# A jump table on TensorE that picks narrower projections in a ragged self-attention kernel

## The chip, the cores and the metric

The kernel runs on one core of one Trainium2 chip. A core has five engines with an instruction stream each: TensorE (PE in the profile, its weight loads PEld), VectorE (DVE), ScalarE (ACT), GpSimd (POOL) and SyncE (SP). Each has a sequencer of its own that also runs register operations, branches and waits on semaphores. DMA engines move data between HBM and the on-chip memory, and they also bring each engine's instructions. The metric is the device time in microseconds (us) of one launch.

## The reference, cut to what matters

`x` holds 32 sequences of up to 512 rows of 512 numbers, 8 heads of 64. Each sequence has a length between 64 and 511, and rows from the length on come out as zero. The lengths are drawn once with a fixed seed; sorted in descending order they are 502, 447, 446, 436, 363, 357, 351, 347, 343, 333, 323, 315, 310, 261, 260, 257, 246, 230, 223, 220, 216, 183, 164, 152, 143, 140, 134, 119, 101, 86, 79, 75.

```python
for b in range(batch):
    seq_len = lengths[b]
    q, k, v = np.split(np.matmul(x[b, :seq_len], w_qkv), 3, axis=-1)
    # per head, scale = 1 / sqrt(64)
    scores = scale * np.matmul(q, k.transpose(0, 2, 1))
    attn = np.exp(scores - scores_max)
    attn = attn / (np.sum(attn, axis=-1, keepdims=True) + 1e-08)
    output[b, :seq_len] = np.matmul(attn, v)
```

## The kernel before, in words

**Head.** `before_loops` sorts the 32 sequences by length on the chip (lines 453 to 530), loads the weights and casts them to 16 bits (`w_r`), and computes the projections of the longest sequence. It also computes, for each loop, up to which pair of sequences it runs (`more`, `counts`, `ends`), and each engine reads these ends into registers (`read_ends`, line 686). DVE fills the masks `alive` and `lower`.

**Loops.** Sorted sequences are taken in pairs, 16 of them. `LOOPS` lists the padded lengths N = 512, 448, 384, 352, ..., 96. Each has one loop in the code, with a body of two positions, j = 0 and j = 1; it goes on while the pair's longer sequence needs more than the next smaller N. With these lengths loop 352 turns three times, 224 and 160 twice, and every other loop once. A loop's end (lines 1543 to 1553) advances registers on every engine and branches back.

**A position.** At position p TensorE works for two sequences at a time: the attention of sequence p, and the projections of sequence p + 1, whose rows lie transposed in `xT`, masked to zero past their length. The order of the steps within a position is written out by hand in `ORDER`, one list for each N (for some N one for each j). For N = 352 it is `L P D S0 S1 S2 V0 K0* V1 S3 S4 S5 A0 V2* K1* S6 S7 S8 A2 Q2* K3* Q1* S9 S10 S11 Q0 A4 Q3* K2* X A6`.

- S: scores, line 1155: matmuls on 64 rows, two heads side by side, N columns. ACT takes the exponential (line 1173).
- Q and K: projections of the next sequence through `project` (line 261): each block of 128 output rows is four matmuls that add up over c = 0 to 3, each N columns wide. They are 32 matmuls a position for every N. ACT (marked `*`) or DVE copies the result (line 1202).
- V (and W): its values, line 272 (1109), four matmuls of 512 columns each.
- A: attention times values, line 1244, many matmuls of 65 columns; DVE divides (lines 1254 to 1263) into `out_nat`.
- L, P, D, X: masks, casts on POOL (line 332), the load of a later sequence, and the transposition of the next `xT` by DMA.

For N of 128 and 96 the Q, K and V steps of the second position stand in a branch (`skip`, line 1459), so that the last sequence projects nothing after it.

**Waits.** `plan_waits` derives from the steps' reads and writes which semaphore each step waits for; PSUM's eight banks are dealt out by `allotted`. A step's instructions are emitted by `emit` and `issue` (the waits at line 1470). In the body each step is emitted once, in the order of the list, for all engines. The width of a projection is N, whatever the length of the next sequence, which is at most N.

Of the kernel before, what the change touches and what calls it, by code (L numbers as in the profile page):

```python
# [17 lines left out]
P = 128  # L18
# [5 lines left out]
class Op:  # L24
# [6 lines left out]
    writes: tuple = ()  # L31
    dma: bool = False
    skip: bool = False


def plan_waits(head, bodies, entries, rare):
# [122 lines left out]
def kernel(  # L159
# [95 lines left out]

        return 1 < tiles(N) and N <= tiles(N) * P - P // 2

    def project(dst, xT, w0, N, part=range(NC)):

        for c in part:  # L260
            last = nc.tensor.matmul(  # L261
                dst[:, 0:N],
                w_r[:, c, w0 : w0 + P],
                xT[:, c, 0:N],
                start=(c == 0),
                stop=(c == NC - 1),
            )
        return last
# [74 lines left out]
    def before_loops():  # L343
# [336 lines left out]
        def read_ends(e, part=None):  # L680
            def load():
                eng = EN[e]
                words = COUNTS // 4
                for g in range(words) if part is None else [part]:
                    packed = eng.alloc_register(f"packed{e}{g}")
                    eng.reg_load(packed, ends_i[0:1, g : g + 1])
                    for v in range(len(LOOPS) - 1):
                        word, bit = counted(v)
                        if word == g:
                            reg = of(ends[v], e)  # L690
                            if bit:
                                eng.reg_alu(reg, packed, bit, op=ALU.logical_shift_right)
                            if bit < 15:
                                eng.reg_alu(reg, reg if bit else packed, 31, op=ALU.bitwise_and)
# [113 lines left out]
        def twos(source):  # L808
# [83 lines left out]
            ("edge", "slen"),  # L892
            ("lower",),
        )
        read_ends("ACT", 2)
        shorten("wk", w_k, D, 0, "POOL")
        shorten("wk", w_k, D, 1, "POOL")
# [77 lines left out]
    def position(N, j, at, ring):  # L975
# [18 lines left out]
        def op(*args, **kw):  # L994
            ops.append(Op(*args, **kw))
# [193 lines left out]
        def qk(name, m0, is_q, act):  # L1189
            k = ring.pop(0)  # L1190
            bank = banks[k]
            ms = slice(m0, m0 + gm)
            buf = (q_bufs if is_q else k_bufs)[o]

            def matmuls():
                for m in range(gm):
                    w0 = (m0 + m) * P + (0 if is_q else D)
                    last = project(bank[:, m * N : (m + 1) * N], xT, w0, N)
                return last

# [8 lines left out]
            op(low, "PE", matmuls, (f"xT{o}",), (f"bk{k}",), skip=ends)  # L1209
# [253 lines left out]
    def issue(v, j, k, op, instead=None):  # L1463
# [14 lines left out]
        elif op.name in sems and last is not None:  # L1478
            last.then_inc(sems[op.name], 16 if op.dma else 1)

    with tc.tile_critical():
        started = [k for k, op in enumerate(head) if op.name in ("row", "col", "wv0", "wv2")]
        for k in started:
            emit("head", 0, k, head[k])
        for name, amount in lead.items():
            amount -= name in ahead
            if amount and name in owner:
                (nc.sync if owner[name] == "DVE" else EN[owner[name]]).sem_inc(
                    sems[name], unit(name) * amount
                )  # L1490
# [22 lines left out]
        here["until"] = nc.sync.alloc_register("until")  # L1513
        for k, op in enumerate(head):
            if k not in started:
                emit("head", 0, k, op)

        for v, N in enumerate(LOOPS):
            for e, eng in EN.items():
                for base, amount in sorted(fixed[v, e], key=lambda f: (f[0] != "posold", f)):  # L1520
                    reg = regs[e][base, amount]
                    if base == "posold":
                        eng.reg_mov(reg, regs[e]["posin", amount])
                        continue
                    eng.reg_mul(reg, rare_pair[e] if base == "rarein" else pair, entered[base])
                    eng.reg_add(reg, reg, amount)
            for k, op in enumerate(entries[v]):
                emit(v, None, k, op)
            for e in final:
                EN[e].reg_sub(final[e], of(ends[v], e), 1)  # L1530
            body, after = f"loop_{N}", f"after_{N}"
            nc.br_lt(pair, ends[v], on_true=body, on_false=after)
            with nc.body(body):
                hints = {}
                for e in ("ACT", "DVE", "POOL", "SP"):
                    EN[e].reg_alu(leave[e], pair, final[e], op=ALU.is_ge)
                    hints[e] = EN[e].mark_branch_hint_location(leave[e])
                p = nc.snap(pair, min_val=0, max_val=B // 2 - 1)
                here.update({e: p * 2 for e in EN}, pair=p, pairs=pair)
                for j in range(2):  # L1540
                    for k, op in enumerate(bodies[v][j]):
                        emit(v, j, k, op)
                nc.regs_add(pair, pair, 1)
                nc.regs_add(own_pair, own_pair, 1)
                if shared(N):
                    for e, reg in rare_pair.items():
                        EN[e].reg_add(reg, reg, 1)
                for e, eng in EN.items():
                    for (base, amount), reg in regs[e].items():
                        if base in raised and (base != "rare" or shared(N)):  # L1550
                            eng.reg_add(reg, reg, raised[base])
                for e, eng in EN.items():
                    back = eng.br_lt(pair, ends[v], on_true=body, on_false=after)
# [41 lines left out]
```

## Time and profile before

| | us |
|---|---|
| median of 3 runs (338.18 to 339.72) | 338.18 |
| span of the profiled execution, first to last instruction | 336.7 |
| TensorE busy | 322.2 |
| ScalarE busy | 264.5 |
| VectorE busy | 210.0 |
| GpSimd busy | 103.6 |
| Q and K projections (line 261), busy | 145.5 |
| V projections (line 272), busy | 72.3 |
| attention times values (line 1244), busy | 74.2 |
| scores (line 1155), busy | 61.2 |

The profiled execution has no time of its own beside its span; its distance to the median of the runs is 1.5 us. In the profile's rows a group reads "line engine operation out<-in xcount | busy us, mean ns of one | idle time of the engine before them and what ended it". Matmuls overlap each other in the pipeline, so a matmul's duration is longer than its distance from the next: four matmuls of 512 columns take 1.04 us from the start of the first to the end of the last, not four times 380 ns. A row of the timeline gives start, time from the first start to the last end, and what ran. The rows of a table by stretches give, after the stretch, its length and the busy time of each engine.

### The profile page before, as it was taken

The page shows a single profiled execution, that of the slowest core. Times are in us where ns is not written, and L with a number is a line of the kernel's source. Part 1 is how long each engine was busy: PE and PEld are TensorE (multiplying, and loading weights), DVE is VectorE, ACT ScalarE, POOL GpSimd, SP SyncE. Part 2 cuts the span into 40 slices and gives each one's busy share as a digit, 9 for nine tenths or more (in the row PEclk, how much of TensorE's full clock was granted, in tenths as well). Part 3 has the DMA queues.
Part 4 walks back from the last instruction along what each step waited for, and adds up shares of the span by engine and source line. Part 5 has one row for each costly group of instructions (what it writes and reads, how often), then busy time and mean ns, then how long its engine had stood idle before and what let it go on. Part 6 is the DMA issues. An engine that isn't in the chain of part 4 may idle for free.

```text
span 336.7 us, 10690 instructions
## 1 busy us (share of the span) xinstructions
PE 322.2 (96%) x3832; PEld 200.0 (59%) x3832; DVE 210.0 (62%) x654; ACT 264.5 (79%) x416; POOL 103.6 (31%) x149
## 2 busy tenths in 40 slices
PE   7999999999999999999999999999999999999881
PEld 4444545554555556556556656665677777678760
DVE  6676666666666564465455457665776656867764
ACT  5388799898978879989989988788567678777651
POOL 5546040504030320330231253043222244244321
PEclk9999999999999999999999999999999999999998
DMA  6974994484637946957947848969946966977671
GB/s 218 391 270 108 324 177 145 121 305 116 207 51 237 318 142 228 288 173 277 300 140 275 239 140 321 258 173 341 262 139 182 204 193 169 207 229 210 219 196 71
DMA packets 72124, 72.08 MB, mean 214 GB/s; under 512 B 41872, under 2 KB 41872, under 8 KB 72080
## 3 DMA queue, kind: packets, MB, share of 16 engines
q1 hardware_dynamic: 72032, 71.52, 71.9%
q8 instruction: 24, 0.39, 0.5%
q14 instruction: 20, 0.16, 0.2%
q10 hardware_dynamic: 48, 0.00, 0.0%
HBM read 28.32 MB, written 33.55 MB: 184 GB/s over the span
## 4 chain that ended last, share of the span: by engine, by line
PE 91%; DVE 3%; DMA 3%; issue 1%; SPq 0%; POOL 0%; ACT 0%; POOLq 0%
PE banks L261 38%; PE banks L272 18%; PE banks L1244 17%; PE banks L1155 16%; PE banks L1109 2%; DMA xT<-x 1%; DMA x_nat<-in_x_dram 1%; DVE out_nat L1263 1%; DVE rcp L1260 1%; PE banks L732 0%; DVE rcp L1254 0%; SPq L609 0%; DVE kT L781 0%; ACT et L1173 0%; DVE x L327 0%
## 5 line engine op out<-in xcount | busy, mean ns | idle before, releaser
L1173 ACT ACTIVATE et<-banks 128x704 f16<-128x704 f32 (+7 forms) x260 | 195.6, 826 | 31.7 <-PE banks L1155 30.3
L261 PE MATMUL banks<-xT,w_r 128*128 128x352 f16 (+11 forms) x1024 | 145.5, 287 | 1.4 <-DMA xT<-x 1.2
L332 POOL TENSOR_TENSOR x<-x_nat,mask 128x512 f16<-128x512 f32 x85 | 86.2, 1039 | 182.9 <-DVE mask L998 170.7
L261 PEld LDWEIGHTS banks<-xT,w_r 128*128 128x128 f16 x1024 | 85.4, 98 | 41.8 <-issue 7.4
L1244 PEld LDWEIGHTS banks<-v_aug,et 128*128 128x128 f16 x1792 | 66.4, 98 | 21.3 <-issue 7.2
L1244 PE MATMUL banks<-v_aug,et 128*128 128x65 f16 x1792 | 74.2, 194 | 0.7 <-ACT et L1173 0.7
L272 PE MATMUL banks<-w_r,xT 128*128 128x512 f16 x284 | 72.3, 380 | 0.6 <-DVE xT L741 0.5
L1263 DVE TENSOR_TENSOR out_nat<-banks,rcp 128x256 f32<-128x256 f32 (+1 forms) x136 | 64.1, 472 | 6.8 <-DMA out_dram<-out_nat 2.2
L1155 PE MATMUL banks<-qz,kT 64*128 64x352 f16 (+11 forms) x640 | 61.2, 298 | 2.9 <-DVE out_nat L1263 2.5
L1254 DVE RECIPROCAL rcp<-banks 128x4 f32<-128x4 f32 (+1 forms) x136 | 25.0, 184 | 44.3 <-PE banks L1244 42.8
L1202 DVE CAST qz<-banks 128x352 f16<-128x352 f32 (+5 forms) x44 | 25.3, 575 | 26.3 <-PE banks L261 25.8
L1155 PEld LDWEIGHTS banks<-qz,kT 64*128 64x128 f16 x640 | 22.6, 94 | 31.8 <-issue 23.4
L272 PEld LDWEIGHTS banks<-w_r,xT 128*128 128x128 f16 x284 | 23.7, 97 | 27.2 <-issue 5.2
L1218 DVE CAST v_aug<-banks 128x512 f16<-128x512 f32 x41 | 28.2, 692 | 16.7 <-PE banks L272 16.6
L1202 ACT CAST kT<-banks 128x352 f16<-128x352 f32 (+5 forms) x58 | 27.6, 478 | 10.2 <-PE banks L261 9.0
L1202 ACT CAST qz<-banks 128x352 f16<-128x352 f32 (+5 forms) x47 | 22.2, 477 | 6.0 <-PE banks L261 4.3
L1202 DVE CAST kT<-banks 128x512 f16<-128x512 f32 (+4 forms) x33 | 19.4, 590 | 7.3 <-PE banks L261 6.9
L1260 DVE TENSOR_TENSOR rcp<-rcp,v_aug 128x4 f32<-128x4 f32 (+1 forms) x108 | 19.6, 181 | 3.7
L1218 ACT CAST v_aug<-banks 128x512 f16<-128x512 f32 x26 | 15.6, 602 | 6.6 <-PE banks L272 6.6
L1074 DVE TENSOR_SCALAR v_aug<-alive 128x24 f16 (+3 forms) x32 | 7.7, 239 | 6.5 <-issue 6.5
L1341 POOL MEMSET kT<- 128x128 f16 (+1 forms) x8 | 1.7, 218 | 28.8 <-PE banks L1155 28.8
L418 PE MATMUL banks<-h_ones 128*128 128x128 f16 (+2 forms) x34 | 5.7, 349 | 1.9 <-POOL h_ones L408 1.9
(81 smaller groups left out, 84.0 us busy)
## 6 DMA issues: line engine op xcount, KB each, us to landing
x_nat<-in_x_dram SPq DMA_DIRECT2D x12, 768.0 KB, 5.5
out_dram<-out_nat SPq DMA_DIRECT2D x12, 768.0 KB, 4.0
x_nat<-in_x_dram SPq DMA_DIRECT2D x14, 512.0 KB, 3.8
x_nat<-in_x_dram SPq DMA_DIRECT2D x7, 1024.0 KB, 6.9
out_dram<-zeros SPq DMA_DIRECT2D x12, 512.0 KB, 5.6
out_dram<-out_nat SPq DMA_DIRECT2D x12, 512.0 KB, 4.5
out_dram<-out_nat SPq DMA_DIRECT2D x4, 1024.0 KB, 4.9
out_dram<-zeros SPq DMA_DIRECT2D x12, 256.0 KB, 5.5
```

The costliest lines, as they stand in the source:

```text
L261: last = nc.tensor.matmul(dst[:, 0:N], w_r[:, c, w0 : w0 + P], xT[:, c, 0:N], start=(c == 0), stop=(c == NC - 1),)
L272: last = nc.tensor.matmul(pv, xT[:, c, t * P : (t + 1) * P], w_r[:, c, 2 * D : 3 * D], start=(c == 0), stop=(c == NC - 1),)
L332: return engine.tensor_tensor(out=x16, in0=x32, in1=live.broadcast_to([P, D]), op=ALU.mult)
L1074: return nc.vector.tensor_scalar(out=v_bufs[o][:, t0:t1, :, HD], in0=table[:, bass.ds(at("DVE") + (j + 1), 1), t0:t1] .rearrange("p o t -> ...
L1155: last = nc.tensor.matmul(psc[par][:, x * wide : x * wide + N], kT[r, i, c0 : c0 + P], qz[r, i, 0:N], start=True, stop=True,)
L1173: return nc.scalar.activation(out=et[:, :, x0:x1, 0:N], in_=got.rearrange("p j (x q) -> p j x q", q=wide)[:, :, x0:x1, 0:N], func=AF.Exp, ...
L1202: return copy_on(act)(out=buf[:, ms, 0:N], in_=bank[:, 0 : gm * N].rearrange("p (m q) -> p m q", q=N),)
L1218: return copy_on(act)(out=v_bufs[o][:, t, :, 0:HD], in_=bank.rearrange("p (h d) -> p h d", d=HD))
L1244: last = nc.tensor.matmul(pav[:, g, qt, :], e_bufs[e][:, c0 + qt * P : c0 + (qt + 1) * P], v_aug[:, kt, h, :], start=(kt == 0), stop=(kt = ...
L1254: return nc.vector.reciprocal(out=rcp, in_=pav[:, :, :, HD])
L1260: return nc.vector.tensor_tensor(out=rcp, in0=rcp, in1=rows, op=ALU.mult)
L1263: return nc.vector.tensor_tensor(out=o_t[:, 0:n, h0 * HD : (h0 + heads) * HD].rearrange("p t (g d) -> p g t d", d=HD), in0=pav[:, :, :, 0:HD],
```

## The change

**A word for each pair.** Nine small DVE operations in the head compute, for each sequence, how many steps of 16 columns the length of the next one lies below its loop's N, at most 3, and pack the two numbers of a pair into one word of `variants`. Two POOL memsets clear the tables. TensorE reads the first word at the end of the head into a register; each second position reads the word of the next pair.

**A jump table in each position.** `emit_position` takes the place of the loop over a position's steps. All engines but TensorE get their steps as before. On TensorE the steps up to the first Q or K block that stands behind some other TensorE step are emitted once; then a `Switch` with four bodies, each of which holds every TensorE step from that block to the last Q or K block (S, V and A steps between them included); then the rest. In body v the matmuls of Q and K for c = 1, 2, 3 are 16v columns narrower than N, while c = 0 keeps the full width, so that every column is written. The columns left out belong to rows of `x` that are zero. Blocks ahead of the `Switch` keep the full width. Positions whose Q and K steps stand in a branch (second positions of 128 and 96) have no `Switch`.

The `Switch` is a jump through a register: a stride times the number of the variant, added to the first body's place. [...] 

```diff
-    def project(dst, xT, w0, N, part=range(NC)):
+    def project(dst, xT, w0, N, part=range(NC), live=None):
         for c in part:
+            width = live if live and c else N
             last = nc.tensor.matmul(
-                dst[:, 0:N],
+                dst[:, 0:width],
                 w_r[:, c, w0 : w0 + P],
-                xT[:, c, 0:N],
+                xT[:, c, 0:width],
...
+    STEP, VARIANTS, FIELD = 16, 4, 2
+    variants = const.tile([P, B // 2 + 1], I32)
...
+        op("kept0", "POOL", lambda: pool.memset(kept, 0), ("order",), ("kept",))
+        op("variants0", "POOL", lambda: pool.memset(variants, 0), ("order",), ("variants",))
+        whole = small("whole", "DVE", ...)      # length + 15
+        op("kept", "DVE", ...)                  # >> 4
+        narrow = small("narrow", "DVE", ...)    # loop of each pair, from `more`
+        wide = small("wide", "DVE", ...)
+        loop_of = small("loop_of", "DVE", ...)
+        loop_at = small("loop_at", "DVE", ...)  # N / 16
+        spare = small("spare", "DVE", ...)      # N / 16 - kept of the next sequence
+        least_of = small("least_of", "DVE", ...)  # at most 3
+        op("variants", "DVE", ...)              # second * 4 + first
...
+        op("word", "PE", lambda: nc.tensor.reg_load(here["variants"], variants[0:1, 0:1]), ("variants",))
...
-                    last = project(bank[:, m * N : (m + 1) * N], xT, w0, N)
+                    last = project(bank[:, m * N : (m + 1) * N], xT, w0, N, live=here["live"])
...
+    def emit_position(v, j):
+        ops, N = bodies[v][j], LOOPS[v]
+        mine = [k for k, op in enumerate(ops) if op.eng == "PE"]
+        blocks = [k for k in mine if ops[k].blocks]
+        first = next((k for k in blocks if any(not ops[i].blocks for i in mine if i < k)), None)
+        if first is None or ops[first].skip:
+            first = last = len(ops)
+        else:
+            last = blocks[-1] + 1
+        here["live"] = N
+        for k, op in enumerate(ops):
+            if op.eng != "PE" or k < first:
+                emit(v, j, k, op)
+        which, word = of(variant, "PE"), here["variants"]
+        def following():
+            if j:
+                nc.tensor.reg_load(word, variants[0:1, bass.ds(here["pair"] + 1, 1)])
+        if first == len(ops):
+            return following()
+        if j:
+            nc.tensor.reg_alu(which, word, FIELD, op=ALU.logical_shift_right)
+        else:
+            nc.tensor.reg_alu(which, word, 2**FIELD - 1, op=ALU.bitwise_and)
+        chosen = nc.snap(variant, min_val=0, max_val=VARIANTS - 1)
+        for at in nc.tensor.Switch(chosen, VARIANTS):
+            here["live"] = max(N - at * STEP, STEP)
+            for k in range(first, last):
+                if ops[k].eng == "PE":
+                    emit(v, j, k, ops[k])
+        following()
+        for k in range(last, len(ops)):
+            if ops[k].eng == "PE":
+                emit(v, j, k, ops[k])
...
-                    for k, op in enumerate(bodies[v][j]):
-                        emit(v, j, k, op)
+                    emit_position(v, j)
```

More of the change, by code (lines that the diff above doesn't have):

```diff
@@ L33 @@
     skip: bool = False
+    blocks: bool = False
 def plan_waits(head, bodies, entries, rare):
@@ L894, in before_loops @@
         )
+        kept = const.tile([P, B + 2], I32, name="h_kept")
+        op("kept0", "POOL", lambda: pool.memset(kept, 0), ("order",), ("kept",))
+        op("variants0", "POOL", lambda: pool.memset(variants, 0), ("order",), ("variants",))
+        whole = small(
+            "whole",
+            "DVE",
+            lambda t: dve.tensor_scalar(
+                out=t, in0=slen, scalar1=float(STEP - 1), scalar2=None, op0=ALU.add
+            ),
+            ("slen",),
+            (P, B),
+            I32,
+        )
@@ new lines, in before_loops @@
+        op(
+            "kept",
+            "DVE",
+            lambda: dve.tensor_scalar(
+                out=kept[:, 0:B],
+                in0=whole,
+                scalar1=STEP.bit_length() - 1,
+                scalar2=None,
+                op0=ALU.logical_shift_right,
+            ),
+            ("whole", "kept"),
+            ("kept",),
+        )
+        passed_by = [[(448 - M) // 32 for M in LOOPS[1:] if LOOPS[LOOPS.index(M) - 1] - M == d] for d in (32, 64)]
+        assert passed_by[0] == list(range(3, COUNTS)) and passed_by[1] == [0, 2]
@@ new lines, in before_loops @@
+        narrow = small(
+            "narrow",
+            "DVE",
+            lambda t: dve.tensor_reduce(
+                out=t, in_=more[:, 3:COUNTS, :].rearrange("p k j -> p j k"), axis=AX.X, op=ALU.add
+            ),
+            ("more",),
+            (P, B // 2),
+        )
+        wide = small(
+            "wide",
+            "DVE",
+            lambda t: dve.tensor_tensor(out=t, in0=more[:, 0, :], in1=more[:, 2, :], op=ALU.add),
+            ("more",),
+            (P, B // 2),
+        )
@@ new lines, in before_loops @@
+        loop_of = small(
+            "loop_of",
+            "DVE",
+            lambda t: dve.scalar_tensor_tensor(
+                out=t, in0=wide, scalar=2.0, in1=narrow, op0=ALU.mult, op1=ALU.add
+            ),
+            ("wide", "narrow"),
+            (P, B // 2),
+        )
+        loop_at = small(
+            "loop_at",
+            "DVE",
+            lambda t: dve.tensor_scalar(
+                out=t,
+                in0=loop_of,
+                scalar1=float(32 // STEP),
+                scalar2=float(LOOPS[-1] // STEP),
+                op0=ALU.mult,
+                op1=ALU.add,
+            ),
+            ("loop_of",),
+            (P, B // 2),
+        )
@@ new lines, in before_loops @@
+        spare = small(
+            "spare",
+            "DVE",
+            lambda t: dve.tensor_tensor(
+                out=t,
+                in0=loop_at.unsqueeze(2).broadcast_to([P, B // 2, 2]),
+                in1=kept[:, 1 : B + 1].rearrange("p (j two) -> p j two", two=2),
+                op=ALU.subtract,
+            ),
+            ("loop_at", "kept"),
+            (P, B // 2, 2),
+        )
+        least_of = small(
+            "least_of",
+            "DVE",
+            lambda t: dve.tensor_scalar(
+                out=t, in0=spare, scalar1=float(VARIANTS - 1), scalar2=None, op0=ALU.min
+            ),
+            ("spare",),
+            (P, B // 2, 2),
+        )
@@ L895, in before_loops @@
+        op(
+            "variants",
+            "DVE",
+            lambda: dve.scalar_tensor_tensor(
+                out=variants[:, 0 : B // 2],
+                in0=least_of[:, :, 1],
+                scalar=float(2**FIELD),
+                in1=least_of[:, :, 0],
+                op0=ALU.mult,
+                op1=ALU.add,
+            ),
+            ("least_of", "variants"),
+            ("variants",),
+        )
         read_ends("ACT", 2)
@@ L1513 @@
         here["until"] = nc.sync.alloc_register("until")
+        here["variants"] = nc.tensor.alloc_register("variants")
+        variant = nc.alloc_registers("variant", engines=[mybir.EngineType.PE])
         for k, op in enumerate(head):
```

2 lines of the change are left out of this document (1 added, 1 removed).

## The prediction

> **What bounds the kernel now.** I read the page first (busy shares, the granted clock, the queues, the chain that ended last), then the groups of instructions by line with shapes kept apart, then the table by stretches, and last TensorE's own order of time in the loop of 352.
>
> ```profile
> span 336.7 us, 10690 instructions
> PE 322.2 (96%) x3832; PEld 200.0 (59%) x3832; DVE 210.0 (62%) x654; ACT 264.5 (79%) x416; POOL 103.6 (31%) x149
> PEclk9999999999999999999999999999999999999998
> q8 instruction: 24, 0.39, 0.5%
> PE 91%; DVE 3%; DMA 3%; issue 1%; SPq 0%; POOL 0%; ACT 0%; POOLq 0%
> PE banks L261 38%; PE banks L272 18%; PE banks L1244 17%; PE banks L1155 16%; PE banks L1109 2%; DMA xT<-x 1%; DMA x_nat<-in_x_dram 1%; DVE out_nat L1263 1%; DVE rcp L1260 1%; PE banks L732 0%; DVE rcp L1254 0%; SPq L609 0%; DVE kT L781 0%; ACT et L1173 0%; DVE x L327 0%
> ```
>
> TensorE is the bound: busy 96%, 91% of the chain, at the full clock, and line 261, the Q and K projections that the change shortens, is the largest share of the chain (38%). So time that TensorE gains or loses inside a loop is nearly time of the kernel.
>
> The next rows give the cost of a column, the state of one stage, and how tight its other engines are.
>
> ```profile
> L261 PE MATMUL banks<-xT,w_r 128*128 128x352 f16 x192 | 33.6, 313 | 0.0
> L261 PE MATMUL banks<-xT,w_r 128*128 128x512 f16 x96 | 23.0, 379 | 0.0
> core 0: us, PE busy (x) PEld busy (x) DVE busy (x) ACT busy (x) POOL busy (x), PEclk, DMA share, GB/s
> 121.34:194.50 73.16, 73.16 (x842) 42.91 (x840) 37.69 (x108) 65.74 (x115) 18.42 (x19) 1.00 0.74 227
> ```
>
> A column costs (379 - 313) / 160 = 0.41 ns. The stretch is the loop of 352: three turns, six positions, 12.19 us each. ACT is at 90% there, so it can follow a faster TensorE only a little.
>
> **What is removed.** With the fixed draw, sorted, the next length gives these variants v (16v columns left out), two positions a pair: loop 512: 3, 3; 448: 0, 3; 384: 1, 2; 352: 0, 0, 1, 1, 2, 2; 320: 3, 3; 288: 1, 2; 256: 1, 2; 224: 0, 0, 2, 3; 192: 2, 3; 160: 1, 1, 2, 3; 128: 2; 96: 1 (in the last two only the first position has a jump). That is 30 jumps: 5 to variant 0, 25 to another. A position has 32 projecting matmuls, 24 of them shortened, so one unit of v is 24 x 16 = 384 columns or 0.158 us. Blocks that stand ahead of the first other TensorE step keep full width (K1, Q1 of 384's first position; K0, K2 of 224; K0 of 192's second). With these taken off, the units add up to 46.5: 46.5 x 0.158 = 7.4 us. As ACT and DVE must follow, I count 6 us, with 0 and 7.4 as ends.
>
> **What is added on TensorE's sequencer.** Ahead of the variants come a register operation, the two values of the stride, a multiplication, an addition and the jump.
>
> ```profile
> L692 PEldq ALU_OP  x3: 36/36/36, 14.6 to 15.0; - x3
> L694 PEldq ALU_OP  x3: 36/36/36, 14.5 to 14.9; - x3
> L1553 PEldq COMPARE_BRANCH  x2: 214/222/231, 145.3 to 169.7; - x2
> L1553 PEldq COMPARE_BRANCH  x3: 67/67/74, 60.3 to 120.9; - x3
> L686 PEldq TENSOR_LOAD <-ends_i x3: 311/318/499, 13.0 to 17.2; - x3
> ```
>
> The six operations of L692 and L694 start between 14.5 and 15.0 us: one in 0.1 us, whatever its 36 ns of work. The two taken back edges in the loop of 352 took 214 and 231 ns, the first three that fell through 67 to 74. So the entry is about 6 x 0.1 + 0.22 = 0.8 us of sequencer time. The exit is another taken jump (0.22 us), and each second position reads the next word (0.31 to 0.50 us).
>
> What covers this is the work already queued on TensorE when its sequencer reaches the jump. In the loop of 352 the order is S0 S1 S2 V0, then the variants from K0 on:
>
> ```profile
> 145.10 0.71 PE L1244 MATMUL banks<-v_aug,et 128*128 128x65 f16 x18
> 145.75 0.62 PE L1155 MATMUL banks<-qz,kT 64*128 64x352 f16 x6
> 146.31 1.04 PE L272 MATMUL banks<-w_r,xT 128*128 128x512 f16 x4
> 147.18 0.76 PE L261 MATMUL banks<-xT,w_r 128*128 128x352 f16 x4
> 157.30 0.71 PE L1244 MATMUL banks<-v_aug,et 128*128 128x65 f16 x18
> 157.94 0.62 PE L1155 MATMUL banks<-qz,kT 64*128 64x352 f16 x6
> 158.50 1.04 PE L272 MATMUL banks<-w_r,xT 128*128 128x512 f16 x4
> 159.37 0.76 PE L261 MATMUL banks<-xT,w_r 128*128 128x352 f16 x4
> L1470 PEldq EVENT_SEMAPHORE  x8: 51/51/51, 121.3 to 194.6; - x8
> ```
>
> The sequencer handles its separate semaphore wait just ahead of S0; from there it issues S and V0 in some 0.2 us (my estimate from the back edge at 145.3, which it has reached while the A matmuls of 145.10 still run). In a first position it restarts about at 145.75, so 1.2 us of matmuls stand before K0 at 147.18; in a second it can run on about when A starts at 157.30 and has up to 1.7 us before K0 at 159.37. Mean 1.45 us: the 0.8 us of entry alone are hidden, with 0.65 us left. Without that cover they would be 30 x 0.8 = 24 us. The exit and the load stand behind full projections (four matmuls of 352 are 0.6 us) and cost nothing or, where few are left, some tenths: 15 loads x 0.1 = 1.5 us; ends 0 and 15 x 0.5 = 7.5.
>
> **The term that decides: code that has to be fetched.** Each variant is a copy of 112 of the 140 matmuls of a 352 position (all but S0 to S2, V0 and the last A6), 224 instructions and more with the weight loads, and four stand one behind the other. The page's row of the instruction queue shows code streaming in while TensorE runs: 24 packets, 0.39 MB, 16 KB each. TensorE runs 2 x 3832 instructions; less the repeats (two turns of 352 at 561, one each of 224 and 160 at about 176 matmuls and as many loads) that is 6,190 different ones, and 0.39 MB over them is 63 bytes each: every piece of 16 KB, some 260 instructions, is fetched once, and a repeated turn fetches nothing. Its price: 0.5% of 16 engines' 336.7 us is 27 us, or 1.1 us a packet, with nobody waiting. A jump past the next piece asks for a packet nobody has ordered. No row shows one. From below it costs the packet alone, 1.1 us. The nearest rows with a start-up are the two smallest loads:
>
> ```profile
> col<-in_lengths_dram ACTq DMA_DIRECT2D x1, 0.2 KB, 1.9
> row<-in_lengths_dram SPq DMA_DIRECT2D x1, 8.0 KB, 2.0
> ```
>
> 2.0 us to land 8 KB, mostly start-up, plus a packet's 1.1 us gives 3.1 us, which I take since a demanded fetch has both. From above: two start-ups and a packet, 2 x 2.0 + 1.1 = 5.1 us.
>
> Variant 0 follows the jump directly; I take it as already on its way, at no cost. For the other 25, 3.1 - 0.65 = 2.45 us of TensorE standing still. Some comes back: a 352 position needs (32 x 352 + 12 x 512 + 12 x 352) x 0.41 ns + 72 x 0.03 us = 11.0 us of its 12.19 (the two row halves of the S matmuls run together), so up to 1.2 us are small waits on ACT and DVE, which catch up during a stall. I give back 0.25, leaving 2.2 us: 25 x 2.2 = 55 us. Ends: 25 x (1.1 - 0.65 - 0.45) = 0 and 25 x (5.1 - 0.65) = 111 us.
>
> [...]
>
> **Back edges.** Four are taken (352 twice, 224 and 160). A turn now holds some ten pieces and touches about eight. If the head is gone, a back edge costs a fetch less the matmuls queued, about 2 us; if not, nothing as now. I take half: 4 us, ends 0 and 4 x 4.5 = 18.
>
> **The start.** DVE gets nine small operations, two memsets go to POOL and a load to TensorE.
>
> ```profile
> 14.39 0.28 DVE L886 TENSOR_TENSOR lower<-h_edge,h_slen 128x128 f32<-128x128 int32 x1
> 16.12 0.69 DVE L781 CAST qz<-banks 128x512 f16<-128x512 f32 x1 [1.45 <-PE banks L261]
> 14.59 1.91 POOL L709 CAST w_r<-w_k 128x512 f16<-128x512 f32 x3 [0.74 <-DMA w_k<-in_w_qkv_dram]
> 22.08 0.99 PE L1155 MATMUL banks<-qz,kT 64*128 64x512 f16 x6 [0.35 <-DVE kT L781]
> ```
>
> Nine at 0.16 to 0.28 us are 1.5 to 2 us, behind "lower", where DVE idles 1.45 us; POOL waits 0.74 us for w_k anyway and TensorE 0.35 us for kT. Zero; were that cover gone, 0.5 us.
>
> **Sum.** Span 336.7 - 6 + 1.5 + 55 + 4 + 0 = 391.2 us. The median of the runs, 338.18, stands 1.5 us over this span, so 392.7; I say 392.
>
> **Rivals.** (1) *The pieces are there already.* If TensorE's memory is filled several pieces ahead, or a fetch takes under the 0.65 us of cover, no jump waits: 338.2 - 6 + 1.5 = 333.7, down to 331. For it: back edges over two pieces cost nothing. Against: 24 packets for 24 pieces show no large lead, and a packet alone takes 1.1 us. Deciding point: the fetch equals the cover; each 0.1 us over it costs 2.5 us, and at 0.25 us over it the gain is gone.
> (2) *Only the sequencer's work is seen.* No fetch waits, but cover is shorter outside 352 and 0.3 us of each of 30 jumps shows: 338.2 - 6 + 9 + 1.5 = 343.
> (3) *The clock falls as well.* In the tail TensorE's last matmul starts near 330.1:
>
> ```profile
> 330.07 0.18 PEld L1244 LDWEIGHTS banks<-v_aug,et 128*128 128x128 f16 x4 [0.21 <-ACT et L1173]
> 330.50:336.70 6.20, 0.00 (x0) 0.00 (x0) 1.58 (x5) 0.00 (x0) 0.45 (x1) 0.81 0.22 86
> ```
>
> A mean of 0.81 over 6.2 us fits half clock for the last 2.4, so about 4 us of idleness suffice. [...] Stalls of 2.45 us stay below; at 4 us each a few us of half speed follow, say 1.5 us lost a time: 25 x (4 - 0.25 + 1.5) = 131, with the other terms 469; where half of them fall so, about 431.
>
> **Chances.** Forecast (fetches wait, 340 to 430) 0.70; rival 1 0.15; rival 2 0.06; rival 3 0.09. The range 339 to 435 leaves out rival 1 and part of rival 3 (0.05). The forecast's own range is 360 to 430. A measurement of this kernel tells 0.5%, 1.7 us, from no change: faster 0.15 (rival 1), same 0.04 (the forecast's low end, where a fetch costs hardly more than its cover), slower 0.81.
>
> **What would show it.** Right: instruction packets well over 24; TensorE idle 2 to 3 us just before the first Q or K block behind V0 in about 25 positions and not in those with v = 0; the loop of 352 longer in its second and third turn than in its first (v = 0, 0); matmuls of L261 in forms 16 to 48 columns narrower; DVE's Q copies at most 0.5 us later. Wrong: gaps of under 0.5 us there (rivals 1 and 2), equal gaps in all 30 (the jump, not the fetch), a PEclk row with digits of 5 to 7 (rival 3).

## The result, and the profile after

The changed kernel takes 557.98 us (median; 551.33 to 563.5) against 338.24 before: a ratio of 1.642 (95% interval 1.633 to 1.651). Slower was forecast, by 54 us; it is 220 us, outside the stated range. The profiled execution is the slowest of the four, at 563.5 us (span 561.7), 1% above the median; its rows are read for where the time lies.

The page of the changed kernel, the lines that answer to those shown of before:

```profile
span 561.7 us, 11070 instructions
PE 382.8 (68%) x3832; PEld 224.8 (40%) x3833; DVE 213.8 (38%) x663; ACT 267.9 (48%) x416; POOL 104.0 (19%) x151
PEclk9988998798896987788889888797877795758775
q8 instruction: 126, 2.06, 1.6%
PE 67%; issue 29%; DVE 2%; POOLq 0%; ACT 0%; POOL 0%; DVEq 0%; SPq 0%
```

and its view by core (span, then mean granted clock):

```profile
core 0: 561.7 us, clock 0.832
```

The 225 us between the spans split in two. TensorE's idle time (span less busy) grew from 14.5 to 178.9 us, by 164; its busy time grew from 322.2 to 382.8, by 61, with the same number of matmuls and fewer columns. The second part is the clock: the record of this execution has only the steps 1.0 and 0.5, and with these a mean of 0.832 is 189 us at half speed. "Issue" in the chain, 29%, is time in which the profile shows nothing that TensorE waits for. Code is fetched 126 times instead of 24.

Where it idles, and who ends it (engine, line, cause, then us in total, times, longest):

```profile
PE banks L264 <- issue: 99.4, 30, 5.8
PE banks L1357 <- issue: 30.7, 16, 4.3
PE banks L1268 <- issue: 28.7, 10, 5.7
PE banks L275 <- issue: 7.6, 5, 3.7
```

Line 264 is the projections. Laid beside the times of the jumps, 28 of its 30 waits are entries into variants, 96 us, 3.4 us each; the other two (0.6 and 3.0 us) belong to blocks ahead of the `Switch` in the loop of 224. The other three rows, 67 us, are A, S and V matmuls: for the most part what stands behind an exit or a back edge. The sequencer's own rows show the jumps (duration in ns, least, median and most; L1622 is the `Switch`, entry and exit, L1705 the back edge). An exit is the jump from a body's last instruction to the common end. A hint at the start of each body announces it, the first at 27.9 us, right behind the first entry; the entries have none:

```profile
L1622 PEldq COMPARE_BRANCH  x60: 295/3341/7189, 24.5 to 546.9; - x60
L1622 PEldq BRANCH_PREFETCH_HINT  x30: 31/40/50, 27.9 to 546.2; - x30
L1705 PEldq COMPARE_BRANCH  x16: 78/82/4080, 70.6 to 556.4; - x16
```

Half of all 60 jumps took 3.3 us or more, up to 7.2. One by one: of the 30 entries 27 took 3.3 us or more, and only 3, all to variant 0, took under 1 us (0.70, 0.41, 0.98); the two others to variant 0 took 4.39 and 3.56. Of the 30 exits 13 took about 0.3 to 0.55 us and 17 took 1.2 to 7.2, nearly all in loops of 288 and below. The back edges of 352 took 3.59 and 3.91 us, that of 224 3.80 and that of 160 4.08. The second turn of 352, in TensorE's order of time:

```profile
193.58 0.62 PE L1268 MATMUL banks<-qz,kT 64*128 64x352 f16 x6 [3.38 <-issue]
194.14 1.04 PE L275 MATMUL banks<-w_r,xT 128*128 128x512 f16 x4
199.07 1.31 PE L264 MATMUL banks<-xT,w_r 128*128 128x352 f16 x4 [3.90 <-issue]
```

The back edge ends in 3.38 us of idleness, S and V0 run, the entry costs 3.90 more, and the four projections after it take 1.31 us instead of 0.76, at a granted clock of 0.50.

Not all of the 166 us of waits on "issue" end with a jump: exits make 37 us and the four back edges 13, and some 21 us, in about a dozen waits, fall where the sequencer simply runs on. In the loop of 288 the wait cuts through a step of 18 matmuls, at a place with no jump:

```profile
318.61 0.68 PE L1357 MATMUL banks<-v_aug,et 128*128 128x65 f16 x17 [0.70 <-issue]
323.61 0.24 PE L1357 MATMUL banks<-v_aug,et 128*128 128x65 f16 x1 [4.31 <-issue]
```

The exit was over at 318.45 us, and one packet of the instruction queue began at 321.2, within the wait. In the first turn of 352 the exit of the first position took only 0.30 us, and yet V0 of the second, a little later, waited 3.75 us. So behind a jump the next piece in order can be missing too.

### The profile page after: what moved, and what is told of

Same layout as the page of the kernel before. It is cut to its first block, busy times and chain, and to the rows that moved or that the text cites. A ratio compares the mean times of both kernels' runs of the same rounds, so it can differ in the third digit from the quotient of the medians.

```text
span 561.7 us, 11070 instructions
## 1 busy us (share of the span) xinstructions
PE 382.8 (68%) x3832; PEld 224.8 (40%) x3833; DVE 213.8 (38%) x663; ACT 267.9 (48%) x416; POOL 104.0 (19%) x151
## 4 chain that ended last, share of the span: by engine, by line
PE 67%; issue 29%; DVE 2%; POOLq 0%; ACT 0%; POOL 0%; DVEq 0%; SPq 0%
PE banks L264 27%; PE banks L275 15%; PE banks L1357 12%; PE banks L1268 11%; PE banks L1222 1%; PE banks L427 1%; DVE out_nat L1376 1%; PE banks L741 0%; DVE rcp L1373 0%; DVE rcp L1367 0%; ACT v_aug L1331 0%; POOLq L695 0%; DVE kT L790 0%; DVE h_loop_of L952 0%; DVE h_spare L975 0%
## 5 line engine op out<-in xcount | busy, mean ns | idle before, releaser
L264 PE MATMUL banks<-xT,w_r 128*128 128x224 f16 (+20 forms) x1024 | 165.3, 318 | 100.8 <-issue 99.4
L264 PEld LDWEIGHTS banks<-xT,w_r 128*128 128x128 f16 x1024 | 96.8, 112 | 151.8 <-issue 122.1
L1357 PE MATMUL banks<-v_aug,et 128*128 128x65 f16 x1792 | 81.3, 201 | 31.6 <-issue 30.7
L275 PE MATMUL banks<-w_r,xT 128*128 128x512 f16 x284 | 91.5, 457 | 8.2 <-issue 7.6
L1357 PEld LDWEIGHTS banks<-v_aug,et 128*128 128x128 f16 x1792 | 72.2, 102 | 58.7 <-issue 47.7
L1268 PE MATMUL banks<-qz,kT 64*128 64x352 f16 (+11 forms) x640 | 69.3, 330 | 30.4 <-issue 28.7
L1268 PEld LDWEIGHTS banks<-qz,kT 64*128 64x128 f16 x640 | 25.7, 102 | 64.8 <-issue 57.3
L275 PEld LDWEIGHTS banks<-w_r,xT 128*128 128x128 f16 x284 | 27.5, 112 | 45.6 <-issue 28.7
L1373 DVE TENSOR_TENSOR rcp<-rcp,v_aug 128x4 f32<-128x4 f32 (+1 forms) x108 | 18.4, 171 | 3.7
```

The lines of the kernel that those rows point to most:

```text
L264: last = nc.tensor.matmul(dst[:, 0:width], w_r[:, c, w0 : w0 + P], xT[:, c, 0:width], start=(c == 0), stop=(c == NC - 1),)
L275: last = nc.tensor.matmul(pv, xT[:, c, t * P : (t + 1) * P], w_r[:, c, 2 * D : 3 * D], start=(c == 0), stop=(c == NC - 1),)
L1268: last = nc.tensor.matmul(psc[par][:, x * wide : x * wide + N], kT[r, i, c0 : c0 + P], qz[r, i, 0:N], start=True, stop=True,)
L1357: last = nc.tensor.matmul(pav[:, g, qt, :], e_bufs[e][:, c0 + qt * P : c0 + (qt + 1) * P], v_aug[:, kt, h, :], start=(kt == 0), stop=(kt = ...
L1373: return nc.vector.tensor_tensor(out=rcp, in0=rcp, in1=rows, op=ALU.mult)
```

## The experiments

### The same code, always the first body

```diff
-            here["live"] = max(N - at * STEP, STEP)
+            here["live"] = N
...
-                out=t, in0=spare, scalar1=float(VARIANTS - 1), scalar2=None, op0=ALU.min
+                out=t, in0=spare, scalar1=0.0, scalar2=0.0, op0=ALU.min, op1=ALU.add
```

> The code of the changed kernel, place for place, but every variant has the full width N and the word is always 0, so that each jump goes to the first body, the piece right behind the jump. Theory A (a jump waits when its target is not the next piece in order, which is fetched ahead): the entries cost 0.4 to 0.7 us each, as those of variant 0 in some first positions did, about 28 entry stalls of 3.3 to 6 us go, and with them most of the half clock; late exits in the loops of 256 and below and the four back edges stay: 380 to 440 us. Theory B (a jump waits whenever its piece was not ordered early enough, and after a jump that was announced nothing is fetched ahead): first positions enter free, second positions still stall 3.3 to 4.5 us, as 4.39 and 3.56 us at variant 0 in second positions of the changed kernel suggest: 440 to 500 us. Rival (the jump through a register itself waits, wherever it goes): 550 to 570 us.

### The same code, always the last body

As above, but with 3.0 added, so that the word is 3.

> The same code again, all variants at full width N, but the word always picks the last body, the farthest from the jump; its exit falls into the next piece. Against the run with the word 0 the distance is the only difference. Theories A and B: all 30 entries stall 3.3 us or more; exits are cheaper than in the changed kernel, since the common end is the next piece in order: 520 to 570 us. Narrowing nothing costs 6 to 7 us against the changed kernel at the full clock, up to 10 with part of it at half clock. Rival (the jump itself waits): the same time as with the word 0 within 10 us.

523.5 us (ratio 1.544, 1.539 to 1.549) with the word 0; 494.3 and 511.2 in the two runs with the word 3, of which the profile shows the second. Who ended TensorE's idleness, with the word 0:

```profile
PE banks L264 <- issue: 56.6, 28, 4.6
PE banks L1357 <- issue: 41.3, 19, 4.3
PE banks L1268 <- issue: 28.7, 12, 6.0
```

and with the word 3:

```profile
PE banks L264 <- issue: 90.6, 26, 6.0
PE banks L1268 <- issue: 12.3, 5, 3.9
PE banks L1357 <- issue: 11.6, 8, 2.3
```

The distance to the target trades places: with the near body less waiting ahead of the projections, where the entries lie (56.6 against 90.6 us), and more ahead of A and S, where exits and back edges lie (70.0 against 23.9). So it is not the jump through a register that waits. But theory A falls: with the word 0, where each target is the next piece, 13 of 14 entries of second positions still took 2.3 us or more, while 8 of 16 in first positions took under 0.9. B says so in kind; both were too low in size there, and too high for the word 3 (520 to 570).

With the word 3 some repeated positions did not wait at all, neither at the entry nor at the exit: the first position of 352's second turn, and both of 224's:

```profile
L1622 PEldq COMPARE_BRANCH  x2: 186/190/193, 190.8 to 200.3; - x2
L1622 PEldq COMPARE_BRANCH  x4: 173/178/193, 385.5 to 393.0; - x4
```

A jump to code that the turn before had brought, in the same body, took 0.17 to 0.19 us. I read this as the plain price of the jump, and the other 3 us and more as the fetch. (It is not so in every repeat: the second position of that same turn of 352 took 6.4 us to enter.) Where no other fetch was under way, a jump took 3.3 us: five entries of the changed kernel took 3.33 to 3.34 us, and in each of them one packet of the instruction queue began 0.9 to 1.0 us behind the start of the jump, the one before it at least 2.8 us ahead of the jump. Pieces further back than two can still be there: in the kernel before, a turn of 352 is about 281 matmuls and 280 loads, more than two pieces of some 260 instructions, and its taken back edges took 0.21 and 0.23 us.

### The narrowing without a jump

```diff
-                    last = project(bank[:, m * N : (m + 1) * N], xT, w0, N)
+                    last = project(..., xT, w0, N, live=N - 16 * LEFT_OUT[N][j])
```

`LEFT_OUT` holds the numbers of this draw's lengths, so this kernel is right for this draw alone.

> The kernel before without any jump: the width of the three later projecting matmuls is written into the code for each loop and position, as the smallest number of columns that this draw's lengths allow to be left out there (48, 48 in 512; 0, 48 in 448; 16, 32 in 384; none in 352 and 224; 48, 48 in 320; 16, 32 in 288 and 256; 32, 48 in 192; 16, 16 in 160; 32 in 128; 16 in 96). That is 34 of the units of 16 columns, all blocks counted. By the prediction's price of 0.158 us a unit it gains 5.4 us at most, and 4.4 with the prediction's discount of 6 to 7.4: 333 to 334.5 us. Rival (the matmul time is not the bound once ACT has to follow): under 1.5 us gained, 337 or more.

334.7 us, ratio 0.987 (0.984 to 0.990): 4.4 us gained, as expected. The trace has 13,824 columns of projections less than before, which is 36 units of 384 and not the 34 expected. So the narrow matmuls are worth 4.4 / 36 = 0.12 us a unit, and 46.5 units 5.7 us, near the prediction's 6.

### Branches within the piece

```diff
+            with nc.tensor.If_lt(which, 2):
+                emit(v, j, k, op)
+            with nc.tensor.Else():
+                here["live"] = N - 2 * STEP
+                emit(v, j, k, op)
```

> The changed kernel's word, but no jump table: each Q or K block stands twice in a row, at full width and 32 columns narrower, and a compare-and-branch on TensorE's sequencer picks by variant 2 and 3 against 0 and 1. Targets are a few instructions away, most in the same piece. Theory (distance to code that is not there makes the stall): no stall over 0.5 us, the clock stays full, 34 units of 16 columns are saved, 5.4 us less a discount, and 8 branches a position of 0.07 to 0.35 us on the sequencer, most of it behind queued matmuls, cost 0 to 4 us: 333 to 338 us. Rival (any branch on TensorE in mid-stream costs what it takes): 200 branches at 0.2 us or more and the lost lead, 355 us or more.

Ratio 0.997 (0.992 to 1.002), and once more, with more rounds:

> The kernel with inline branches once more, with more rounds, to settle its sign: the first time its ratio was 0.9967 with an interval of 0.9919 to 1.0016. In its trace 258 branches took 43 us of sequencer time and none over 0.4 us, the loops with variants 2 and 3 were 0.3 to 0.6 us a turn shorter than before and those with 0 and 1 were 0.1 to 0.3 us longer. Theory (the narrowing's gain, less a tenth or so of a us for each position's branches): 0.994 to 0.999. Rival (no difference): an interval that holds 1.

1.000 (0.998 to 1.002): no difference. Its page:

```profile
PE 318.2 (94%) x3832; PEld 198.3 (59%) x3833; DVE 213.1 (63%) x663; ACT 263.9 (78%) x416; POOL 104.2 (31%) x151
PEclk9999999999999999999999999999999999999998
```

and the sequencer's rows of its branches:

```profile
L1611 PEldq COMPARE_BRANCH  x258: 65/179/496, 24.4 to 326.8; - x129
```

258 branches, none over 0.5 us, and the full clock: branching in mid-stream is not what costs. But nothing is won either. The 258 branches belong to 129 blocks and took 43 us of the sequencer, 0.33 us a block, while a block of 352 becomes only 3 x 32 x 0.41 ns = 0.04 us shorter.

Fewer branches, one for each run of neighbouring blocks:

> As the run with inline branches, but Q and K blocks that follow each other on TensorE share one branch: 5 branches instead of 8 in a position of 352. The same 34 units of 16 columns are saved, so what is not gained of the static kernel's 4.4 us is the price of branches on the sequencer. Theory (each branch takes its 0.2 to 0.35 us out of the sequencer's lead, and some of it shows): it gains more than the inline run, 335 to 337 us, ratio 0.988 to 0.996. Rival (the branches are hidden and the gap to the static kernel comes from elsewhere, such as ACT's wait for banks): no difference to the inline run, ratio 0.996 to 0.998.

Ratio 1.007 (1.005 to 1.009): slower than with all the branches. The expectation falls. There are 157 branches here in place of 258, so the price does not go with their number; why longer arms cost more is open.

### Announcing the jump

```diff
+            nc.tensor.switch_hint(chosen, VARIANTS, label=label)
         for k in mine:
             if k < first:
                 emit(v, j, k, ops[k])
-        for at in nc.tensor.Switch(chosen, VARIANTS):
+        for at in nc.tensor.Switch(chosen, VARIANTS, hint=label):
```

> The changed kernel with one thing added: the jump into the variants is announced, by a hint with the variant's number at the start of each position's code on TensorE. Theory (the entry stall is the time of one fetch of 3.4 us, started at the jump, plus any fetch still under way): a hint that stands t ahead shortens the stall by t. First positions reach the jump 0.8 to 1.5 us after their start and keep 2 to 3.5 us; second positions reach it 2 to 6 us after the exit of the first and keep 0 to 1.5 us. Together some 55 us less idleness and 10 to 20 us less half clock: 470 to 510 us; exits and back edges as before. Rival (the wait is the jump's own, or the sequencer does nothing else while it fetches): 545 to 570 us.

549.2 us, ratio 1.623 (1.619 to 1.627): almost nothing, and within the rival's range. The idleness ahead of line 264 fell, the rest rose:

```profile
PE banks L264 <- issue: 74.9, 30, 5.1
PE banks L1357 <- issue: 38.4, 17, 3.6
PE banks L1268 <- issue: 34.6, 17, 4.7
```

The lead was misjudged: the sequencer goes from the hint to the jump in 0.5 to 2.9 us (5.9 in one place), since it runs ahead of the matmuls. The first hint stands at 23.92 us, the jump at 24.77, and it took 2.83 us instead of 3.41, 0.6 us less with a lead of 0.85. Over all 30 places the lead is 1.4 us on average, but the entries fell only from 3.84 to 3.39 us, so the theory does not hold in general. So I put the variants later, at the fourth block:

```diff
+        if first is not None and len(blocks) > 4:
+            first = blocks[3]
-        if first is None or ops[first].skip:
+        if first is None or ops[first].skip or not (tiles(N) > 2):
```

> As the run with announced jumps, but the variants begin only at the fourth Q or K block, and only loops of 288 and above have a jump table (16 jumps; every projection elsewhere at full width). The hint then stands 4 us or more ahead of the jump and the bodies are long enough for the exit's hint. Theory: no entry or exit stalls over 1 us; the back edges of 352 still fetch, two times 3.5 to 4 us and some half clock after them; 2.7 us are saved: 338 to 350 us. Rival (jumps between pieces cost even when announced, one fetch at a time being too slow for three pieces a position): 370 us or more.

433.8 us, ratio 1.282 (1.275 to 1.289). Its entries and exits, and its back edges:

```profile
L1631 PEldq COMPARE_BRANCH  x32: 303/2102/4783, 28.6 to 329.3; - x32
L1715 PEldq COMPARE_BRANCH  x16: 70/85/4282, 68.1 to 428.2; - x16
```

Of 16 announced entries 9 took 0.5 us or less and 6 took 3.1 to 4.8, although their hints stood 2.3 to 9.6 us ahead; 14 of 16 exits took 0.9 us or more, although announced at the body's start. An announcement can work, but here it often had no effect. In the changed kernel's trace 108 of the 125 distances between the starts of two packets of the instruction queue are 3.0 us or more, so an announced piece may lose its place to a piece fetched in order; that is a guess, and the cause stays open.

### One jump alone

```diff
-        if first is None or ops[first].skip:
+        if first is None or ops[first].skip or (N, j) != (320, 1):
```

> The changed kernel with one jump table alone, in the second position of 320 (variant 3), all other positions as before, with all of the new head and the register loads. Theory: one entry stall of 3.4 to 5 us, of which about 0.4 us is covered, and one window of 3.4 us at half clock behind it, which costs up to 1.7 us; 0.5 us saved by the narrow matmuls; nothing for the exit, the loads and the head: 3 to 6 us over the kernel before, ratio 1.009 to 1.018. Rival (the head's added work or the fifteen loads cost something too): 8 us or more.

Ratio 1.036 (1.034 to 1.038), 12.6 us: outside the expectation, on the side of its rival. By the starts of the back edges, the loop of 320 is 7.5 us longer and each turn of 352 0.6; this kernel has the register load at the very end of a turn, with little queued behind it. So I took the other loads out:

> As the run with one jump table in the second position of 320, but the register loads of the other positions are gone: one load stands at the end of 320's first position. In the trace of the run before, the loop of 320 took 7.5 us longer than in the kernel before (its entry waited 6.72 us: a fetch in order had begun 0.3 us ahead of the jump and the demanded one began 4.6 us after that), and the loops of three and four tiles 0.5 us longer a turn. Theory (that second part is the load at the end of a turn, where only the last A matmuls cover it): 6 to 8 us over the kernel before, ratio 1.018 to 1.024. Rival (the added head or the moved code costs it): 11 to 13 us over, as with the loads.

347.8 us, ratio 1.028 (1.025 to 1.030): 9.2 us, a little over the expectation, below its rival. The turns of 352 are as long as before again, so the load was what they lost. By the starts of the back edges 1.1 us are lost ahead of the loop of 352, before the jump, 7.0 in the loop of 320 and 1.0 in the next; so the jump itself costs about 8 us. Its page:

```profile
PE 324.6 (94%) x3832; PEld 200.7 (58%) x3833; DVE 211.6 (61%) x663; ACT 264.7 (76%) x416; POOL 103.8 (30%) x151
PEclk9999999999999999999999996999999999999996
```

the sequencer's row of the two jumps, entry and exit:

```profile
L1622 PEldq COMPARE_BRANCH  x2: 336/3130/5925, 207.1 to 223.5; - x2
```

and TensorE in the order of time around them:

```profile
207.04 1.04 PE L1222 MATMUL banks<-w_r,last_xT 128*128 128x512 f16 x4
213.22 3.01 PE L264 MATMUL banks<-xT,w_r 128*128 128x320 f16 x12 [5.14 <-issue]
```

The entry took 5.93 us. The packets of the instruction queue began at 207.5 and 210.7 us and the jump at 207.1: I read this as a fetch in order that was just starting, which the demanded one had to follow. TensorE idles 7.3 us more than before in this execution (346.4 - 324.6 = 21.8 against 14.5), and one slice of the clock row falls to 6: the 12 projections after the stall take 3.01 us.

### Idleness without a fetch

To see whether it is the stall or the fetch that brings the clock down, the kernel before got nothing but semaphore increments at the 30 places of the jumps.

```diff
+            if k == first:
+                for _ in range(20):      # 40 in the other run
+                    nc.tensor.sem_inc(passed, 1)
```

> The kernel before with no variants and no jump: at the 30 places where the changed kernel has its jump, 20 semaphore increments on TensorE's sequencer, some 1.5 to 2 us with no code fetched. Theory (TensorE loses what its queue doesn't cover; idle stretches well under 3.4 us leave the clock alone): 0.5 to 1.2 us a place: 353 to 375 us, the granted clock as before outside the tail.

> The same with 40 increments a place, 2.9 to 4 us of sequencer time, about what the entry into a variant takes. Theory (idle stretches of 3 us and more halve the clock for the next 3.4 us and more): 2 to 3.2 us a place of plain idleness, 60 to 96 us, and on top of that slow matmuls in many places, 10 to 40 us: 410 to 475 us, more than twice the loss of the run with 20. Rival (the clock falls for another reason than idleness, the code fetches for one): 400 to 435 us at the full clock.

407.3 and 413.6 us in two runs (the profile shows the first), and 552.9 us, ratio 1.633 (1.630 to 1.636). Both are over their ranges: an increment took the sequencer 0.15 us (from the first of 20 to the last 2.9 us, of 40 5.9 us), twice what I had expected, so the places last 3.0 and 6.05 us. The short one, by its page and by core:

```profile
PE 331.5 (82%) x3832; PEld 204.2 (50%) x3832; DVE 209.1 (52%) x654; ACT 267.3 (66%) x416; POOL 103.6 (26%) x149
PEclk9999999999999999999998899999999999898997
q8 instruction: 25, 0.41, 0.4%
```

```profile
core 0: 405.4 us, clock 0.973
```

and the long one, in the same views:

```profile
PE 388.8 (70%) x3832; PEld 231.1 (42%) x3832; DVE 209.6 (38%) x654; ACT 269.1 (49%) x416; POOL 103.6 (19%) x149
PEclk9979888887977997898879878877787777777776
q8 instruction: 27, 0.44, 0.3%
```

```profile
core 0: 551.8 us, clock 0.829
```

The long run has about the changed kernel's time, clock and idleness (163.0 us against 178.9) with hardly a fetch more than before. That the two times agree so well is luck, since the places came out twice as long as planned. What it shows is that stalls of the sequencer are enough for a loss of this kind and size, half clock included, and that the clock needs no fetch to fall. The idleness grew by 59.4 and 148.5 us, 2.0 of 3.0 and 4.95 of 6.05 us a place: queued matmuls cover 1.0 to 1.1 us. And the clock goes with the length of a stall: idle times of 2.0 us on average (1.1 to 3.0) cost 9 us of slow matmuls in all, those of 5 us cost 67. In the changed kernel the first entry already did it: TensorE idled 2.82 us there, and the clock was 0.50 for the 3.4 us behind it (the third number from the end in the second row):

```profile
28.04 3.29 PE L264 MATMUL banks<-xT,w_r 128*128 128x512 f16 x8 [2.82 <-issue]
28.10:31.50 3.40, 3.40 (x10) 1.08 (x12) 0.82 (x2) 0.00 (x0) 2.90 (x3) 0.50 0.42 82
```

The record of that execution has 30 stretches at half speed. They last 3.4, 6.8, 10.2 or 13.7 us, multiples of 3.41, but for the last, which the end cuts off; the run with one jump has one of 6.8 us. A limit of 3.4 us of idleness, as the short run's expectation has it, no run shows: here 2.82 us were enough, and the short run lost 9 us with 1.1 to 3.0 us a place.

## Why the prediction was wrong

The direction and the mechanism held (a jump to code that is not there waits for a fetch, TensorE stands still, nothing makes up for it); what failed are terms of the sum. The slow matmuls, 66 us, were put at nothing and left to a rival; exits were put at nothing; code in order behind a jump was not in the sum; and the entries were too low by 41 us.

| term | predicted, us | measured, us |
|---|---|---|
| narrow matmuls | -6 | -5.7 (0.12 a unit, by the static kernel) |
| entries: idleness | 55 | 96, in 28 waits ahead of line 264 |
| exits and back edges: idleness | 4 | 50 (37 and 13) |
| code in order behind a jump: idleness | 0 | about 21 |
| slow matmuls | 0 | 61 more busy time, 66 with the narrowing's 5.7 |
| register loads, head | 1.5 | not told apart; 0.6 us a load where only the last A matmuls cover it |

- *Which jumps wait.* That all 25 jumps past the next piece find their code missing was an assumption that no row of the kernel before shows; in the changed kernel all 25 took 3.3 us or more.
- *The price of a fetch.* "3.1 us, which I take" was near for a fetch that starts at once: 3.3 us. But a fetch can find another under way, as at the single jump (5.9 us); the 30 entries took 3.84 us on average. Fetches one after the other were not in the sum.
- *"Variant 0 follows the jump directly; I take it as already on its way, at no cost."* Two of five waited 3.6 and 4.4 us, and 13 of 14 second positions in the run that always took body 0. This step failed, and in the same way the code in order behind an exit or a back edge was sometimes missing.
- *The cover.* 1.45 us of queued matmuls were counted, mean of two positions of 352; over all 30 places it is 1.0 to 1.1. Of the 0.25 us given back per stall little came: the waits add up to 166 us and the idle time grew by 164.
- *"The exit and the load ... cost nothing or, where few are left, some tenths."* For the jump of the exit it holds where the body runs for some 9 us, in 352 and 320 (0.3 to 0.5 us). But 17 exits took 1.2 us or more, 15 of them in the short bodies of 288 and below; that the announced end is not there yet is the likely reason. The step looked at the jump's own 0.22 us and not at the fetch of its target, which the same section had priced for the entry.
- *Back edges.* "I take half": all four waited, 3.6 to 4.1 us.
- *The clock.* "Stalls of 2.45 us stay below" set it at nothing. Rival 3, with a chance of 0.09, was right that it falls, and needed no second fetch in a row for it: the first entry, 3.4 us, was enough. Its 469 us are still 89 too low. It priced slow matmuls at 1.5 us a stall, an estimate that no run shows; the long idle run has 67 / 30 = 2.2.
- *A count.* The 6,190 different instructions take off only one of the repeats of 224 and 160; with both it is about 5,840, or 67 bytes each. The reading, that every piece is fetched once, stays.

Rival 1 is out: entries idle 96 us. Rival 2 is out as the whole: 258 branches within the piece cost only about what their narrowing gains, 34 x 0.12 = 4.2 us.

Of the signs named for being right, these came: packets well over 24 (126), gaps in front of the first block, longer second and third turns of 352. Of the signs of being wrong, the clock row with 5 to 7 came. The forecast gave the loop of 352 a free first turn (v = 0, 0), and its second position waited.

## What to carry to other kernels

On TensorE, count the sequencer's stall and not the jump: a jump to code not yet on the chip stops the sequencer for 3.3 us or more while only 1 us of matmuls is queued, and where TensorE idles long enough (2.8 us did it once here, 2 us mostly not) the clock behind is halved as well. Duplicated bodies have four places to miss (the way in, the way out, the loop's way back, and the next piece in order behind any of them), and each is priced with a fetch of its own, two in a row where fetches meet (5.9 us at the single jump). A saving of 0.04 us a block did not pay for a branch either: here only widths written into the code gained (1.3%), and those hold for one draw.

## What the runs showed of the hardware that I had not expected

- Code from the turn before can still be there: jumps into such a body took 0.17 to 0.19 us.
- After an announced jump, even the next piece in order may not be there: 13 of 14 entries of second positions waited with the word 0, and in the changed kernel a step was cut in two by 4.3 us where nothing jumps.
- An announcement 2.3 to 9.6 us ahead was often without effect (6 of 16 entries); not explained.
- A semaphore increment on TensorE takes its sequencer 0.15 us.
- 30 plain stalls of 6 us, with no code fetched for them, take the old kernel to 553 us and its clock to 0.829.
